# Extra rows of an expert in two parts of 64 rows instead of four of 32, and no branch prefetch

## The chip, the cores and the metric

The kernel runs on one core of one Trainium2 chip. Its time is the device time of one launch in microseconds; a smaller one is better. The engines are named as in the profile: PE is TensorE's matrix work, PEld its loads of stationary operands, DVE is VectorE, ACT is ScalarE, POOL is GpSimd, SP is the queue that issues most transfers. A `q` behind the name (PEq, PEldq) is the engine's sequencer, which reads the program, takes branches and waits on semaphores.

## The reference

One decoder block over 1024 tokens of width 1024, batch 1: a LayerNorm, three token mixers (gated DeltaNet, mLSTM, latent attention) that are gated, added and projected, a residual LayerNorm, and then a mixture of 16 experts with another residual LayerNorm. The change concerns the experts alone:

```python
scores = sigmoid(x_flat @ router_w)                 # 1024 tokens, 16 experts in 4 groups
# one group per token, the two best experts inside it; weights normalised over the two
for e in range(16):                                  # what routed_experts amounts to
    rows = tokens that chose e                       # as many as there are, no capacity
    y[rows] += w[rows, e] * ((silu(x[rows] @ w1[e]) * (x[rows] @ w3[e])) @ w2[e])
x = layer_norm(DEEPNORM_ALPHA * x + y)
```

There are 2048 pairs of token and expert, so an expert has 128 rows on average; w1 and w3 are 1024x512, w2 is 512x1024, all in float32.

## The kernel before

The front of the kernel (LayerNorm, mixers, merge, output projection, routing) takes the first 1380 us or so and is not touched, but for constants that `route_consts` prepares. Then `experts` runs over the experts in order, e = 0 to 15.

**Main rows.** The first 128 rows of an expert are one block. `turn_a` transposes the gathered rows `xg` and splits them in a high and a low half; `layer1` (8 steps c, one for each 128 inputs) multiplies them with w1 and w3, `layer2` (4 steps) with w2. Each step is six matmuls of 128x512 through `mm_pair` (L1571 to 1576). The weights come from memory by SP in tiles of 128x1024 (`Weights.load`), and ACT and DVE split each tile in a high and a low half (`split`, L1629 and L1630). Tiles are handed back as steps end, and that lets SP load the next.

**Extra rows.** Rows 128 to 255 of an expert are handled in parts of 32 rows, NM = 4 of them. The 32 rows are gathered as 128 lines of 256 numbers: partition 32q + r holds quarter q of row r (`quarters`, `gather` into `k.xm[:, m]`). `part_x` transposes them, `part_1` multiplies them in plain float32 with the unsplit weight tiles, `part_act` is the gate, `part_h` turns the result, `part_2` is the second layer, `part_y` scales and adds the rows to memory. In `part_1` and `part_2` a quarter of TensorE's columns (32 of 128) does a quarter of the output columns: four matmuls with the same 32-column stationary operand, 256 moving columns each, written to partitions 32q to 32q + 31 of the bank tile.

**Branches.** How many rows an expert has is known only at run time. `per_part` (L1696) reads the count once into a register (`count_of`, L1693) and nests one `If(count > 128 + 32 m)` per part, so the code of all four parts is in the program of every expert and what is not needed is jumped over. At the end of the nest the sequencer waits for its own engine. For `part_1` and `part_2` a hint (`ahead`, L1706) tells TensorE's sequencer ahead of time which way a branch will go.

**Order.** The order on PE, DVE and ACT is written by hand in the tables AT0 (expert 0), AT (1 to 14) and LAST (the last two): at step c of expert e, after that step's matmuls, the listed functions are called. In AT, `part_1(e)` comes at step 0, `turn_a(e+1)` and `part_2(e-1)` at step 3 (and there `ahead_1` of e + 1, which is the first to read that expert's count), `part_h(e)` at 4, `part_y(e-1)` at 5, `part_x(e+1)` at 8. POOL's order in this phase is the planner's.

Of the kernel before, what the change touches and what calls it, by code (L numbers as in the profile page):

```python
# [19 lines left out]
P = 128  # L20
# [1271 lines left out]
NE = 16  # L1292
NM = 4
CAPA = 2 * P
# [19 lines left out]
def route_consts(k, pool):  # L1314
# [10 lines left out]
    k.sc = pool.tile([P, NB, NE], F32, name="sc")  # L1325
    k.xm = pool.tile([P, NM, 2 * P], F32, name="xm")
    io = k.xm[:, 0]
    nc.gpsimd.iota(io, pattern=[[1, 2 * P]], base=1, channel_multiplier=0, allow_small_or_imprecise_dtypes=True)
# [12 lines left out]
    nc.gpsimd.memset(k.rowmul[:, 0:1], 1.0)  # L1341
    nc.gpsimd.memset(k.rowmul[:, 1:], 4.0)
    nc.gpsimd.memset(k.rowadd[:, 0:1], 0.0)
    for q in range(4):
        nc.gpsimd.memset(k.rowadd[32 * q:32 * q + 32, 1:], float(q))
    nc.vector.tensor_scalar(k.trash[:, 0:1], pc, float(T), None, op0=OP.add)
    nc.vector.tensor_scalar(k.trash[:, 1:], k.rowadd[:, 1:], -128.0, 4.0 * T, op0=OP.mult, op1=OP.add)
    nc.vector.scalar_tensor_tensor(k.trash[:, 1:], pc.to_broadcast([P, NM]), 4.0, k.trash[:, 1:], op0=OP.mult,
                                   op1=OP.add)
    k.past = pc  # L1350
    nc.vector.tensor_scalar(pc, pc, float(NE * CAPA + 1), None, op0=OP.add)
    k.spread = pool.tile([P, NM, 4, 32], BF, name="spread")
    nc.gpsimd.tensor_copy(k.spread, k.identb.rearrange("p (m r) -> p m r", r=32)[:, :, None, :].to_broadcast(
        [P, NM, 4, 32]))
    blank = k.xm[:, 1].bitcast(I32)[:, :NE * CAPA // P * 4].rearrange("p (j c) -> p j c", c=4)
# [167 lines left out]

def quarters(x):
    return x.rearrange("t (q n) -> (t q) n", q=4)

# [155 lines left out]
def experts(k, ws):  # L1682
# [4 lines left out]
    A = {}  # L1687
    xq, rq = quarters(k.x1), quarters(k.x1r)

# [5 lines left out]

    def per_part(e, fn, eng=nc.tensor, name=None):  # L1696
        count = count_of(e, eng)
        with ExitStack() as st:
            for m in range(NM):
                label = f"{name}_{e}_{m}" if name else None  # L1700
                st.enter_context(tc.If(count > P + 32 * m, label=label))
                if name and m + 1 < NM:
                    ahead(e, name, m + 1)
                fn(m)

    def ahead(e, name, m=0):  # L1706

        tc.mark_branch_hint_location(f"{name}_{e}_{m}", hint=count_of(e, nc.tensor) > P + 32 * m, engines=[ENG.PE])

    def look():  # L1710

        t = k.oh.rearrange("p b n -> p (b n)").bitcast(I32)
        t0 = t[:, :NE * 4].rearrange("p (e c) -> p e c", c=4)
        tq = t[:, NE * 4:NE * 4 * (1 + NM)].rearrange("p (e m c) -> p e m c", m=NM, c=4)
        ds = [nc.sync.dma_start(t0, k.table[:NE * CAPA].rearrange("(e s) c -> s e c", s=CAPA)[:P])]
        for q in range(4):
            for m in range(NM):
                ds.append(nc.sync.dma_start(tq[32 * q:32 * q + 32, :, m], k.table[:NE * CAPA].rearrange(
                    "(e s) c -> s e c", s=CAPA)[P + 32 * m:P + 32 * m + 32]))
        for d in ds:  # L1720
            for w in k.written:
                tc.add_manual_dep(d.ins, w.name, mybir.DependencyInfo(mybir.DependencyClass.Sync,
                                                                      mybir.DependencyReason.DATA),
                                  reason="the table is whole")
        A["table"] = t0, tq, t[:, NE * 4 * (1 + NM):NE * (4 + 6 * NM)].rearrange("p (i e m) -> p e m i", i=2, m=NM)

    def looked():
        t0, tq, iq = A["table"]
        nc.vector.tensor_scalar(iq, tq[:, :, :, 0:2], 4.0, k.rowadd[:, 1:2], op0=OP.mult, op1=OP.add)
# [33 lines left out]
    with tc.tile_pool(name="moe", bufs=2) as pool:  # L1763
        ws.late = pool
        ws.more(k.xsp, ["xs6", "xs7"], 0)
        ws.more(pool, [f"wl_{i}" for i in range(NSLOT - NEARLY - NB)], 0)
        bank = k.pe.tile([P, NM, 512], F32, name="bank")

# [41 lines left out]
        def part_x(e):  # L1810
            a = A[e]

            def turn(m):
                for j in range(2):
                    nc.tensor.transpose(bank[:, m, 256 + j * P:256 + j * P + P], k.xm[:, m, j * P:j * P + P], k.ident)

            per_part(e, turn)
            a.xT = pool.tile([P, NM, 256], F32, name="xmT")
            nc.scalar.activation(a.xT, bank[:, :, 256:], AF.Copy)

        def part_1(e):
            a = A[e]
            keys = [(e, 1, c) for c in range(KD)]
            w = [t.rearrange("p (i q n) -> p i q n", i=2, q=4) for t in ws.whole(keys)]

            def mul(m):
                for c, t in enumerate(w):
                    x = a.xT[:, m, c % 2 * P + c // 2 * 32:c % 2 * P + c // 2 * 32 + 32]
                    for q in range(4):
                        nc.tensor.matmul(bank[32 * q:32 * q + 32, m, 0:256], x, t[:, :, q], start=(c == 0),  # L1830
                                         stop=(c == KD - 1))

            per_part(e, mul, name="p1")
            ws.dropped(keys)

        def part_act(e):
            a = A[e]
            a.hm = pool.tile([P, NM, P], F32, name="mhm", bufs=1)
            silu_mul(k, a.hm, bank[:, :, 0:P], bank[:, :, P:2 * P])

        def part_h(e):
            a = A[e]
            per_part(e, lambda m: nc.tensor.transpose(bank[:, m, 0:P], a.hm[:, m], k.ident))
            a.hT = pool.tile([P, NM, P], F32, name="hmT", bufs=1)
            nc.scalar.activation(a.hT, bank[:, :, 0:P], AF.Copy)

        def part_2(e):
# [4 lines left out]
            def mul(m):  # L1852
                for c in range(4):
                    for q in range(4):
                        nc.tensor.matmul(bank[32 * q:32 * q + 32, m, 256:], a.hT[:, m, 32 * c:32 * c + 32],
                                         w[c][:, 256 * q:256 * q + 256], start=(c == 0), stop=(c == 3))

            per_part(e, mul, name="p2")
            ws.dropped(keys)

        def part_y(e):
            a = A[e]
            o = pool.tile([P, NM, 256], F32, name="mom", bufs=1)
            nc.vector.tensor_tensor(o, bank[:, :, 256:], bc(a.wq, 256), OP.mult)
            per_part(e, lambda m: add_rows(k, rq, a.rq[:, m:m + 1], o[:, m]), nc.gpsimd)

        def last_two(d, e):
# [13 lines left out]
            def whole():  # L1881
                s, bs = norm.tile(), norm.tile(12)
                for i in range(2):
# [9 lines left out]
                   "part_h": lambda: part_h(e), "part_2": lambda: part_2(e), "part_y": lambda: part_y(e),  # L1893
                   "ahead_1": lambda: ahead(e, "p1"), "ahead_2": lambda: ahead(e, "p2"),
                   "ahead_d": lambda: ahead(d, "p2"), "split": lambda: ws.split(min(1, ws.loaded - ws.made)), "layer1": lambda: mul(layer1, e), "act": lambda: act(e),
                   "turn2": lambda: turn2(e), "layer2": lambda: mul(layer2, e, False),
                   "consts": lambda: norm.consts(ws.spare), "gather": lambda: gather(k, z, k.x1r, a.i0), "whole": whole}
            for name in LAST.split():
# [8 lines left out]
               "part_1": part_1, "part_act": part_act, "part_h": part_h, "part_2": part_2, "part_y": part_y, "act": act,  # L1907
               "turn2": turn2, "ahead_1": lambda n: ahead(n, "p1"), "ahead_2": lambda n: ahead(n, "p2")}

# [5 lines left out]
        with tc.manual_schedule(engines=MANUAL):  # L1915
# [6 lines left out]
            for m in range(NM):  # L1922
                nc.scalar.activation(bank[:, m].rearrange("p (c n) -> p c n", n=P), bh(k.ident, 4), AF.Copy, scale=0.0)
            for e in range(NE - 1):
# [11 lines left out]

AT0 = ((-1, "mark", 1), (0, "find", 1), (1, "part_x", 0), (1, "ahead_1", 0), (2, "found", 1), (2, "fetch", 1),
       (2, "part_1", 0), (2, "ahead_1", 1), (5, "part_act", 0), (6, "part_h", 0),
       (7, "act", 0), (7, "turn_a", 1), (7, "part_x", 1), (6, "look", 0), (8, "looked", 0),
       (8, "fetch", 2))  # L1940
# [137 lines left out]
MIX_SCALE = ()  # L2078
LAST = """turn2_d split part_1 ahead_d split*2 part_2_d split part_y_d ahead_2 split part_act layer2_d*2 split part_h split part_2
layer2_d part_y layer2_d layer1*2 consts split*3 layer1*2 load7 split*2 load6 layer1 load0 load4 load3  # L2080
# [385 lines left out]
```

## Time and profile before

| | us |
|---|---|
| median of 3 runs | 1889.41 (1887.40 to 1893.02) |
| profiled execution | 1894.58 |
| its span, first to last instruction | 1892.8 |
| PE busy over the span | 1705.7 (90%) |
| DVE, ACT, POOL busy | 1130.4, 694.5, 384.3 |
| mean granted clock of TensorE | 0.956 of full |

The profiled execution is 1.8 us longer than its span and 5.2 us over the median of the runs. Busy time is a mean over stages: the experts' stage begins near 1380 us and is read in stretches of its own, each from the first layer-1 matmul of one expert to that of another. A branch counts as busy for no engine; its time shows as idle time of PE with the sequencer named as what ended it, or with `issue`, when the profile shows nothing that was waited for.

### The profile page before, as it was taken

Reading aid. Unit: us, or ns where it says so; the run is one execution under the profiler, and the core shown is the slowest. Engines: PE = TensorE matmul, PEld = TensorE weight load, DVE = VectorE, ACT = ScalarE, POOL = GpSimd, SP = SyncE. Lnnn points to the kernel's source line nnn. Section 1 sums busy time; section 2 is a strip of 40 time slices with the busy share of each in tenths; the row PEclk is TensorE's granted clock in tenths of the full one; section 3 lists DMA queues with packets and bytes.
Section 4 is the critical chain, followed back from the end, with each engine's and each line's share of the span. In section 5 each row is a group of like instructions: output and inputs, shape, how many; then the busy total and the mean of one; then the engine's idle time right before and its main releaser. Section 6 shows DMA issues by size and latency. Waiting matters only on the chain. (4 is left out here: it accounts for less than half of the span.)

```text
span 1892.8 us, 28732 instructions
## 1 busy us (share of the span) xinstructions
PE 1705.7 (90%) x10550; PEld 1434.4 (76%) x10550; DVE 1130.4 (60%) x2124; ACT 694.5 (37%) x1157; POOL 384.3 (20%) x419
## 2 busy tenths in 40 slices
PE   6999999999999999999999899979658888889872
PEld 5978988999998888888777788869535556667651
DVE  7685554464455524444576647765855556889766
ACT  6222222112211223345344522212134445778653
POOL 3140212113211005532100200120052212211115
PEclk9999999999999999999999999989879998999996
DMA  7222532323332225442200355371657677999835
GB/s 241 90 90 100 160 121 92 125 87 115 91 106 85 90 80 172 134 128 107 63 13 18 128 178 192 99 219 68 215 153 239 196 230 218 330 312 372 300 96 200
DMA packets 225793, 286.55 MB, mean 151 GB/s; under 512 B 48495, under 2 KB 153961, under 8 KB 225609
## 3 DMA queue, kind: packets, MB, share of 16 engines
q1 hardware_dynamic: 216792, 258.58, 41.4%
q0 software_dynamic: 8816, 25.47, 5.5%
q8 instruction: 122, 2.00, 0.5%
q14 instruction: 63, 0.51, 0.1%
HBM read 214.81 MB, written 69.17 MB: 150 GB/s over the span
## 5 line engine op out<-in xcount | busy, mean ns | idle before, releaser
L360 PE MATMUL psp<-xH,wh 128*128 128x512 f32 x704 | 285.0, 405 | 0.0
L361 PE MATMUL psp<-xL,wh 128*128 128x512 f32 x704 | 274.7, 390 | 3.9 <-POOL ci L509 2.2
L362 PE MATMUL psp<-xH,wl 128*128 128x512 f32 x704 | 276.0, 392 | 0.0
L360 PE MATMUL psp<-wh,xH 128*128 128x256 f32 (+1 forms) x576 | 165.7, 288 | 0.0
L362 PE MATMUL psp<-wh,xL 128*128 128x256 f32 (+1 forms) x576 | 162.4, 282 | 0.0
L361 PE MATMUL psp<-wl,xH 128*128 128x256 f32 (+1 forms) x576 | 162.4, 282 | 0.0
L361 PEld LDWEIGHTS psp<-xL,wh 128*128 128x128 f32 x704 | 132.6, 188 | 30.7 <-POOL ci L509 2.6
L362 PEld LDWEIGHTS psp<-xH,wl 128*128 128x128 f32 x704 | 132.1, 188 | 29.3
L360 PEld LDWEIGHTS psp<-xH,wh 128*128 128x128 f32 x704 | 132.7, 188 | 24.2
L1575 PE MATMUL ph<-wl,xgH 128*128 128x512 f32 x274 | 89.3, 436 | 39.4 <-issue 25.8
L360 PEld LDWEIGHTS psp<-wh,xH 128*128 128x128 f32 x576 | 110.5, 192 | 0.2
L361 PEld LDWEIGHTS psp<-wl,xH 128*128 128x128 f32 x576 | 110.5, 192 | 0.1
L362 PEld LDWEIGHTS psp<-wh,xL 128*128 128x128 f32 x576 | 110.3, 192 | 0.0
L346 DVE TENSOR_TENSOR wl<-wr,wh 128x1024 fp32r<-128x1024 f32 (+1 forms) x62 | 76.0, 1244 | 52.9 <-ACT wh L345 40.9
L1575 PEld LDWEIGHTS ph<-wl,xgH 128*128 128x128 f32 x274 | 54.4, 207 | 57.4 <-issue 38.4
L345 ACT ACTIVATE wh<-wr 128x1024 fp32r<-128x1024 f32 (+1 forms) x62 | 64.0, 1048 | 75.1 <-PE psp L361 51.3
L360 PE MATMUL pwo<-woh,mH 128*128 128x256 f32 x256 | 75.7, 296 | 14.2 <-DVE xs L2182 14.1
L360 PE MATMUL pbr<-yH,brh 128*128 128x512 f32 x192 | 76.5, 398 | 0.5 <-ACT ay L1249 0.5
L361 PE MATMUL pbr<-yL,brh 128*128 128x512 f32 x192 | 76.3, 397 | 0.0
L362 PE MATMUL pbr<-yH,brl 128*128 128x512 f32 x192 | 76.0, 396 | 0.0
L362 PE MATMUL pwo<-woh,mL 128*128 128x256 f32 x256 | 74.0, 289 | 0.0
L361 PE MATMUL pwo<-wol,mH 128*128 128x256 f32 x256 | 74.0, 289 | 0.0
(856 smaller groups left out, 4092.2 us busy)
## 6 DMA issues: line engine op xcount, KB each, us to landing
wl<-in_moe_w_dram SPq DMA_DIRECT2D x126, 256.0 KB
wr<-in_w_in_dram SPq DMA_DIRECT2D x60, 512.0 KB
xs<-in_moe_w_dram SPq DMA_DIRECT2D x82, 256.0 KB
wl<-in_moe_w_dram SPq DMA_DIRECT2D x34, 512.0 KB
gates<-gt SPq DMA_DIRECT2D x24, 512.0 KB
mgt<-gates SPq DMA_DIRECT2D x48, 256.0 KB
we<-in_moe_w_dram SPq DMA_DIRECT2D x48, 256.0 KB
we<-in_moe_w_dram SPq DMA_DIRECT2D x18, 512.0 KB
```

The source lines that it names most:

```text
L345: k.nc.scalar.activation(h, raw, AF.Copy)
L346: k.nc.vector.tensor_sub(l, raw, h)
L360: k.nc.tensor.matmul(out, aH, bH, start=start, stop=False)
L361: k.nc.tensor.matmul(out, aH, bL, start=False, stop=False)
L362: k.nc.tensor.matmul(out, aL, bH, start=False, stop=stop)
L1575: k.nc.tensor.matmul(ps, xL if p == 2 else xH, wl if p == 1 else wh, start=first and p == 0, stop=last and p == 2)
```

## The change

Parts of 64 rows, two of them (NM = 2, R = 64 rows, WP = 512 numbers of a row per line). The 64 rows are gathered as 128 lines of 512 numbers, half q of row r on partition 64q + r. In `part_1` and `part_2` half of TensorE's columns does half of the output columns: two matmuls with a 64-column stationary operand and 512 moving columns each. `part_x` transposes four blocks a part instead of two, `part_h` two instead of one. The bank tile, the gathered tile and the evictions have the same number of elements in all. `ahead` and its entries in the tables go, and with them the hints; the count of an expert is then first read in `part_x`. `look`, which reads the table of rows back, issues 4 transfers instead of 16 beside its first one.

```diff
-NM = 4
+NM = 2
+R = 128 // NM
+WP = 1024 // NM
@@ per_part
-    def per_part(e, fn, eng=nc.tensor, name=None):
+    def per_part(e, fn, eng=nc.tensor):
         count = count_of(e, eng)
         with ExitStack() as st:
             for m in range(NM):
-                label = f"{name}_{e}_{m}" if name else None
-                st.enter_context(tc.If(count > P + 32 * m, label=label))
-                if name and m + 1 < NM:
-                    ahead(e, name, m + 1)
+                st.enter_context(tc.If(count > P + R * m))
                 fn(m)
-
-    def ahead(e, name, m=0):
-
-        tc.mark_branch_hint_location(f"{name}_{e}_{m}", hint=count_of(e, nc.tensor) > P + 32 * m, engines=[ENG.PE])
@@ experts
-        bank = k.pe.tile([P, NM, 512], F32, name="bank")
+        bank = k.pe.tile([P, NM, 2 * WP], F32, name="bank")
@@ part_x
-                for j in range(2):
-                    nc.tensor.transpose(bank[:, m, 256 + j * P:256 + j * P + P], k.xm[:, m, j * P:j * P + P], k.ident)
+                for j in range(WP // P):
+                    nc.tensor.transpose(bank[:, m, WP + j * P:WP + j * P + P], k.xm[:, m, j * P:j * P + P], k.ident)
@@ part_1
-                    x = a.xT[:, m, c % 2 * P + c // 2 * 32:c % 2 * P + c // 2 * 32 + 32]
-                    for q in range(4):
-                        nc.tensor.matmul(bank[32 * q:32 * q + 32, m, 0:256], x, t[:, :, q], start=(c == 0),
+                    x = a.xT[:, m, c % (KD // NM) * P + c // (KD // NM) * R:][:, :R]
+                    for q in range(NM):
+                        nc.tensor.matmul(bank[R * q:R * q + R, m, 0:WP], x, t[:, :, q], start=(c == 0),
                                          stop=(c == KD - 1))
-            per_part(e, mul, name="p1")
+            per_part(e, mul)
@@ part_h
-            per_part(e, lambda m: nc.tensor.transpose(bank[:, m, 0:P], a.hm[:, m], k.ident))
+
+            def turn(m):
+                for j in range(WP // 2 // P):
+                    nc.tensor.transpose(bank[:, m, j * P:j * P + P], a.hm[:, m, j * P:j * P + P], k.ident)
+
+            per_part(e, turn)
@@ part_2
-                    for q in range(4):
-                        nc.tensor.matmul(bank[32 * q:32 * q + 32, m, 256:], a.hT[:, m, 32 * c:32 * c + 32],
-                                         w[c][:, 256 * q:256 * q + 256], start=(c == 0), stop=(c == 3))
-            per_part(e, mul, name="p2")
+                    for q in range(NM):
+                        nc.tensor.matmul(bank[R * q:R * q + R, m, WP:], a.hT[:, m, c % (4 // NM) * P + c // (4 // NM) * R:][:, :R],
+                                         w[c][:, WP * q:WP * q + WP], start=(c == 0), stop=(c == 3))
+            per_part(e, mul)
@@ the tables
-AT = ((0, "part_1", 0), (0, "turn2", -1), (0, "ahead_2", -1), (1, "part_act", 0), (3, "turn_a", 1), (3, "part_2", -1),
-      (3, "ahead_1", 1), (4, "part_h", 0), (5, "part_y", -1), (7, "act", 0),
+AT = ((0, "part_1", 0), (0, "turn2", -1), (1, "part_act", 0), (3, "turn_a", 1), (3, "part_2", -1),
+      (4, "part_h", 0), (5, "part_y", -1), (7, "act", 0),
       (8, "part_x", 1), (9, "fetch", 2))
...
```

AT0 and LAST lose their `ahead` entries in the same way, and the constants of `route_consts`, `look` and `looked` follow NM and R.

## Rows read from the trace of the kernel before

**Rows 1.** Busy time by stretch: expert 0, 1 to 5, 6 to 13, 11 alone, 14 to 15.

```profile
core 0: us, PE busy (x) PEld busy (x) DVE busy (x) ACT busy (x) POOL busy (x), PEclk, DMA share, GB/s
1381.90:1418.20 36.30, 23.42 (x148) 15.65 (x148) 17.70 (x33) 16.40 (x22) 21.77 (x20) 0.80 0.48 99
1418.20:1601.30 183.10, 151.57 (x1209) 107.23 (x1210) 98.42 (x103) 84.57 (x105) 39.15 (x24) 0.92 0.73 219
...
1601.30:1776.50 175.20, 156.27 (x708) 119.59 (x707) 155.25 (x161) 136.15 (x169) 33.43 (x19) 0.98 0.99 339
1714.00:1734.50 20.50, 18.96 (x86) 14.56 (x85) 19.32 (x21) 17.05 (x22) 3.82 (x2) 1.00 1.04 370
1776.50:1837.10 60.60, 42.91 (x309) 29.60 (x308) 34.69 (x35) 27.75 (x35) 7.05 (x4) 0.89 0.51 141
```

**Rows 2.** Waits, 1380 to 1837 us: total us, times, longest us.

```profile
PE ph L1575 <- issue: 29.6, 8, 10.2
PE phT L1550 <- PEq L1698: 16.2, 9, 4.4
...
PE ph L1575 <- PEq L1698: 7.9, 9, 3.6
PE py L1575 <- PEq L1698: 7.7, 8, 4.4
```

**Rows 3.** Branches of L1698 in four stretches: ns min/median/max, first and last start.

```profile
L1698 PEldq COMPARE_BRANCH  x70: 65/176/5262, 1419.2 to 1599.5; - x70
...
L1698 PEldq COMPARE_BRANCH  x18: 82/318/5643, 1605.4 to 1692.0; - x18
...
L1698 PEldq COMPARE_BRANCH  x12: 252/405/526, 1697.6 to 1753.5; - x12
...
L1698 PEldq COMPARE_BRANCH  x21: 70/181/5432, 1780.2 to 1831.8; - x21
```

**Rows 4.** Timeline of PE, part_1 of expert 1: start us, us, what, how many.

```profile
1420.00 1.50 PE L1830 MATMUL bank<-xs,xmT 128*32 128x256 f32 x24
1421.32 2.34 PE L1830 MATMUL bank<-wl,xmT 128*32 128x256 f32 x40
1423.48 1.48 PE L1830 MATMUL bank<-xs,xmT 128*32 128x256 f32 x24
```

**Rows 5.** L1830 alone: expert 1, expert 3, all; then L1855, all; L1815.

```profile
1418.20:1455.40 37.20, 7.11 (x128) 4.06 (x128) 0.91 0.78 236
1492.10:1533.10 41.00, 10.96 (x192) 6.93 (x192) 0.92 0.66 190
...
1381.90:1837.10 455.20, 42.51 (x704) 23.14 (x704) 0.93 0.78 245
...
1381.90:1837.10 455.20, 21.26 (x352) 10.95 (x352) 0.93 0.78 245
...
L1815 PE MATMUL bank<-ident,xm x22: 270/272/273, 1387.1 to 1804.8; 128*128 128x128 f32 x22
```

**Rows 6.** Timeline: the gap behind part_2 in expert 10; the count's load.

```profile
1701.99 0.72 PE L1575 MATMUL ph<-wl,xgH 128*128 128x512 f32 x2 [1.14 <-ACT xgH L1556]
...
L1693 PEldq TENSOR_LOAD <-cnt x16: 306/312/499, 1385.5 to 1794.7; - x16
```

**Rows 7.** Timeline of PE around branches: a short gap, four matmuls at either clock.

```profile
1414.69 0.73 PE L1575 MATMUL ph<-we,xgH 128*128 128x512 f32 x2 [0.43 <-PEq L1698]
...
1436.67 1.18 PE L1575 MATMUL ph<-wl,xgH 128*128 128x512 f32 x4 [1.50 <-issue]
...
1442.17 2.07 PE L1575 MATMUL ph<-wl,xgH 128*128 128x512 f32 x4 [3.64 <-PEq L1698]
...
1650.01 1.09 PE L1550 MATMUL phT<-ident,mhh 128*128 128x128 f32 x4 [2.84 <-PEq L1698]
```

**Rows 8.** DMA queue of TensorE's program: packets, MB, share of 16 engines.

```profile
q8 instruction: 122, 2.00, 0.5%
```

**Rows 9.** Timeline of POOL: the gathers for expert 1.

```profile
1406.92 1.85 POOL L1529 DMA_INDIRECT xm<-x,idx  x1 [0.30 <-issue]
1409.08 0.95 POOL L1529 DMA_INDIRECT xg<-x,idx  x1 [0.31 <-issue]
```

More of the change, by code (lines that the diff above doesn't have):

```diff
@@ L1341, in route_consts @@
     nc.gpsimd.memset(k.rowmul[:, 0:1], 1.0)
[L1342 removed]
+    nc.gpsimd.memset(k.rowmul[:, 1:], float(NM))
     nc.gpsimd.memset(k.rowadd[:, 0:1], 0.0)
[L1344 to L1345 removed]
+    for q in range(NM):
+        nc.gpsimd.memset(k.rowadd[R * q:R * q + R, 1:], float(q))
     nc.vector.tensor_scalar(k.trash[:, 0:1], pc, float(T), None, op0=OP.add)
[L1347 to L1348 removed]
+    nc.vector.tensor_scalar(k.trash[:, 1:], k.rowadd[:, 1:], -128.0, float(NM * T), op0=OP.mult, op1=OP.add)
+    nc.vector.scalar_tensor_tensor(k.trash[:, 1:], pc.to_broadcast([P, NM]), float(NM), k.trash[:, 1:], op0=OP.mult,
                                    op1=OP.add)
@@ L1521, in places, with pieces @@
     yield idx, w
-def quarters(x):
-    return x.rearrange("t (q n) -> (t q) n", q=4)
+def pieces(x):
+    return x.rearrange("t (q n) -> (t q) n", q=NM)
 def gather(k, x, src, idx):
@@ L1687, in experts @@
     A = {}
-    xq, rq = quarters(k.x1), quarters(k.x1r)
+    xq, rq = pieces(k.x1), pieces(k.x1r)
     def count_of(e, eng):
@@ L1715, in look @@
         ds = [nc.sync.dma_start(t0, k.table[:NE * CAPA].rearrange("(e s) c -> s e c", s=CAPA)[:P])]
-        for q in range(4):
+        for q in range(NM):
             for m in range(NM):
-                ds.append(nc.sync.dma_start(tq[32 * q:32 * q + 32, :, m], k.table[:NE * CAPA].rearrange(
-                    "(e s) c -> s e c", s=CAPA)[P + 32 * m:P + 32 * m + 32]))
+                ds.append(nc.sync.dma_start(tq[R * q:R * q + R, :, m], k.table[:NE * CAPA].rearrange(
+                    "(e s) c -> s e c", s=CAPA)[P + R * m:P + R * m + R]))
         for d in ds:
@@ L1728, in looked @@
         t0, tq, iq = A["table"]
-        nc.vector.tensor_scalar(iq, tq[:, :, :, 0:2], 4.0, k.rowadd[:, 1:2], op0=OP.mult, op1=OP.add)
+        nc.vector.tensor_scalar(iq, tq[:, :, :, 0:2], float(NM), k.rowadd[:, 1:2], op0=OP.mult, op1=OP.add)
         for e in range(2, NE):
@@ L1823, in part_1 @@
             keys = [(e, 1, c) for c in range(KD)]
-            w = [t.rearrange("p (i q n) -> p i q n", i=2, q=4) for t in ws.whole(keys)]
+            w = [t.rearrange("p (i q n) -> p i q n", i=2, q=NM) for t in ws.whole(keys)]
             def mul(m):
                 for c, t in enumerate(w):
-                    x = a.xT[:, m, c % 2 * P + c // 2 * 32:c % 2 * P + c // 2 * 32 + 32]
-                    for q in range(4):
-                        nc.tensor.matmul(bank[32 * q:32 * q + 32, m, 0:256], x, t[:, :, q], start=(c == 0),
+                    x = a.xT[:, m, c % (KD // NM) * P + c // (KD // NM) * R:][:, :R]
+                    for q in range(NM):
+                        nc.tensor.matmul(bank[R * q:R * q + R, m, 0:WP], x, t[:, :, q], start=(c == 0),
                                          stop=(c == KD - 1))
-            per_part(e, mul, name="p1")
+            per_part(e, mul)
             ws.dropped(keys)
@@ L1853, in mul @@
                 for c in range(4):
-                    for q in range(4):
-                        nc.tensor.matmul(bank[32 * q:32 * q + 32, m, 256:], a.hT[:, m, 32 * c:32 * c + 32],
-                                         w[c][:, 256 * q:256 * q + 256], start=(c == 0), stop=(c == 3))
-            per_part(e, mul, name="p2")
+                    for q in range(NM):
+                        nc.tensor.matmul(bank[R * q:R * q + R, m, WP:], a.hT[:, m, c % (4 // NM) * P + c // (4 // NM) * R:][:, :R],
+                                         w[c][:, WP * q:WP * q + WP], start=(c == 0), stop=(c == 3))
+            per_part(e, mul)
             ws.dropped(keys)
@@ L1893, in last_two @@
                    "part_h": lambda: part_h(e), "part_2": lambda: part_2(e), "part_y": lambda: part_y(e),
-                   "ahead_1": lambda: ahead(e, "p1"), "ahead_2": lambda: ahead(e, "p2"),
-                   "ahead_d": lambda: ahead(d, "p2"), "split": lambda: ws.split(min(1, ws.loaded - ws.made)), "layer1": lambda: mul(layer1, e), "act": lambda: act(e),
+                   "split": lambda: ws.split(min(1, ws.loaded - ws.made)), "layer1": lambda: mul(layer1, e), "act": lambda: act(e),
                    "turn2": lambda: turn2(e), "layer2": lambda: mul(layer2, e, False),
@@ L1907, in experts @@
                "part_1": part_1, "part_act": part_act, "part_h": part_h, "part_2": part_2, "part_y": part_y, "act": act,
-               "turn2": turn2, "ahead_1": lambda n: ahead(n, "p1"), "ahead_2": lambda n: ahead(n, "p2")}
+               "turn2": turn2}
         def events(table, e, c):
@@ L1922, in experts @@
             for m in range(NM):
-                nc.scalar.activation(bank[:, m].rearrange("p (c n) -> p c n", n=P), bh(k.ident, 4), AF.Copy, scale=0.0)
+                for i in range(0, 2 * WP, 512):
+                    nc.scalar.activation(bank[:, m, i:i + 512].rearrange("p (c n) -> p c n", n=P), bh(k.ident, 4), AF.Copy,
+                                         scale=0.0)
             for e in range(NE - 1):
@@ L1934, in experts @@
             last_two(NE - 2, NE - 1)
-AT0 = ((-1, "mark", 1), (0, "find", 1), (1, "part_x", 0), (1, "ahead_1", 0), (2, "found", 1), (2, "fetch", 1),
-       (2, "part_1", 0), (2, "ahead_1", 1), (5, "part_act", 0), (6, "part_h", 0),
+AT0 = ((-1, "mark", 1), (0, "find", 1), (1, "part_x", 0), (2, "found", 1), (2, "fetch", 1),
+       (2, "part_1", 0), (5, "part_act", 0), (6, "part_h", 0),
        (7, "act", 0), (7, "turn_a", 1), (7, "part_x", 1), (6, "look", 0), (8, "looked", 0),
        (8, "fetch", 2))
-AT = ((0, "part_1", 0), (0, "turn2", -1), (0, "ahead_2", -1), (1, "part_act", 0), (3, "turn_a", 1), (3, "part_2", -1),
-      (3, "ahead_1", 1), (4, "part_h", 0), (5, "part_y", -1), (7, "act", 0),
+AT = ((0, "part_1", 0), (0, "turn2", -1), (1, "part_act", 0), (3, "turn_a", 1), (3, "part_2", -1),
+      (4, "part_h", 0), (5, "part_y", -1), (7, "act", 0),
       (8, "part_x", 1), (9, "fetch", 2))
@@ L2078 @@
 MIX_SCALE = ()
-LAST = """turn2_d split part_1 ahead_d split*2 part_2_d split part_y_d ahead_2 split part_act layer2_d*2 split part_h split part_2
+LAST = """turn2_d split part_1 split*2 part_2_d split part_y_d split part_act layer2_d*2 split part_h split part_2
 layer2_d part_y layer2_d layer1*2 consts split*3 layer1*2 load7 split*2 load6 layer1 load0 load4 load3
```

26 lines of the change are left out of this document (13 added, 13 removed).

## The prediction

> **What bounds the kernel now.** I cut the experts' stage into stretches and read the busy times of each [rows 1]. In an expert without extra rows (expert 11) PE works 18.96 us of 20.50; DVE, at 19.32 us, is as full, and the transfers run at 370 GB/s. Experts 1 to 5 all have extra rows: 183.1 us, 36.6 each, while DVE works only 98.4 us in all and the transfers are at 219 GB/s. There PE alone sets the pace, with 151.6 us of work and 31.5 us of idle time. So in these stretches, and in the last two experts (17.7 us idle in 60.6), a microsecond of PE's work or idle time is a microsecond of the kernel.
>
> The waits tell what the idle time is [rows 2]. The lines ended by PEq L1698, the sequencer at a branch, make 16.2 + 7.9 + 7.7 = 31.8 us, and 29.6 us are "issue", the longest 10.2 us: nothing was waited for, PE had no instruction. The branches themselves show it [rows 3]: the median is 0.2 to 0.4 us, but the longest in three of four stretches take 5.3, 5.6 and 5.4 us, whereas in 1693 to 1755 none is over 0.53. A branch lands either on code that is there or on code that must be fetched; the second costs some 5 us of the sequencer. Part of that is covered, because the sequencer runs ahead of PE: the branch of 5.64 us left PE idle for 2.84 [rows 3, 7]. I put the stalls down to jumps over long code. One part is 64 loads and 64 matmuls in part_1 (704 matmuls for 11 parts [rows 5]) and half of that in part_2, so an expert without extra rows jumps over 512 and 256 instructions. With the change these are 128 and 64.
>
> **The change, term by term.** The sum is made on the profiled execution, 1894.6 us.
>
> *PE's work in the parts.* Line 1830 has 704 matmuls; 64 are one part (128 in expert 1, 192 in expert 3), and line 1815's 22 transposes, two a part, agree: 11 parts, two in expert 1, three in expert 3, six single ones [rows 5]. In parts of 64 rows, expert 1 needs one and expert 3 two: 9. A part of part_1 takes 3.48 us, from 1420.00 to 1423.48 for 64 matmuls [rows 4], that is 0.218 us for each four, though one lasts 0.38: the four quarters run side by side. A part after has 32 matmuls of 512 columns; if two halves run side by side, 16 pairs at twice 0.218 us make 6.96 us. Part_2 is half of it: 1.74 us, then 3.48. So 9 x (6.96 + 3.48) = 94.0 us, with 0.3 us a part for the ends of the two groups 96.7, against the measured 42.51 + 21.26 = 63.8 [rows 5]: +33. Transposes: 14 more in part_x and 7 more in part_h at about 0.11 us spacing make +2. Expert 0's share (6.96 + 0.2 after, 5.8 before) goes into its own term, which leaves **+34**. A 64-column matmul with two halves is not in the trace. The nearest row from below is the quarters' (the 34), from above the same matmuls one behind the other, as if halves did not overlap: 94 us more. I take the former, since what keeps four groups of columns going at once is the same thing.
>
> *Idle time of experts 1 to 5 and of the last two.* With a jump of 64 or 128 instructions where there were up to 512, I expect landings to be as in 1693 to 1755. Then an expert with parts keeps about 0.4 us from the reference expert (1.54 less the 1.14 of the next term) and two or three gaps like the 0.43 us behind part_h [rows 1, 6, 7], 1.5 in all: 31.5 - 5 x 1.5 = **-24**. In the last two, part_1 and part_2 have three such stalls of up to 4.4 us [rows 2]; 17.7 falls to some 6.7: **-11**. The price of a landing is bounded by rows at 0.25 and 5.64 us; I take the lower end, with 1 us a part of slack.
>
> *Experts 6 to 13.* Idle time is 175.2 - 156.3 = 18.9 us [rows 1], of which eight times the reference's 1.54 is 12.3; the other 6.6 are missed landings and should go. In the reference 1.14 us is one gap [rows 6]: behind part_2 the sequencer reads the next expert's count for the hint, and that load alone is 0.31 us of it. The trace names ACT as releaser, but the gap is there in each such expert, with the same count load in it. The change moves the load to part_x, where the sequencer is ahead of six matmuls (1.4 us), so it is hidden; if PE were out of matmuls there, it costs its 0.9 again. Eight times 0.9 would be 7 us; but DVE needs 19.32 us an expert, and the transfers are at 370 GB/s, so only part can be had. I take 4.5. Together **-11**.
>
> *Clock.* [...] Granted clock short of 1 times length is 0.08 x 183.1 + 0.02 x 175.2 + 0.11 x 60.6 = 24.8 us [rows 1], some of it in idle time. With the long gaps gone I take back less than half: **-11**, with 0 and 20 as bounds.
>
> *Expert 0.* 10.2 us of stall follow its part_1 [rows 2], but what comes behind is bound elsewhere: expert 1's rows are gathered at 1409.08, behind POOL's writes of the row table and two part gathers [rows 9]. One of those two goes (expert 1 then has one part), so the gather starts 2.2 us earlier. I take **-4**.
>
> *At nothing.* The evictions have as many elements as before. Gathers and additions move 128 lines of 2 KB in 9 parts for 1 KB in 11, under 3 MB more in 455 us at 245 GB/s [rows 5]. `look` issues 12 transfers fewer on SP ahead of weight loads, which in expert 1 are not what PE waits for. If that cover goes, all three are in favour of the change or under 3 us.
>
> Sum: 34 - 24 - 11 - 11 - 11 - 4 = -27. The profiled 1894.6 becomes 1868; on the median of the runs, 5.2 us lower, **1862 us**.
>
> The program of TensorE is fetched in 122 packets of 2.00 MB [rows 8], 16 KB each. [...]
>
> **Rivals.**
> *Landings still miss, and now nothing is hinted* (slower). Its place is the two jumps of every expert. For it: most experts' jumps hit with hints in 1693 to 1755, and no row shows a long jump without one. Against it: the jumps are a quarter as long, and branches of part_x and part_h, never hinted, are mostly among the short ones. Price: the idle and clock terms (-24, -11, -11 for missed landings and clock, and -6.6) stay away, and 16 unhinted jumps in experts 6 to 13 at up to 2.84 us add some 25: 1889 + 34 + 25 - 8 = about 1940 at full strength; it turns the sign when more than half of the landings miss. At three quarters, 1915.
> *Half of the landings miss or come late*: gains and work cancel, 1886 to 1892.
> *The halves don't run side by side*: 94 us more, 1862 + 94 = 1956. Against it: the quarters do.
> *DVE and the transfers set the floor sooner*, so that experts 1 to 5 gain two thirds and 6 to 13 only the missed landings: 1862 + 15 = 1877. For it: 370 GB/s and 19.32 of 20.50 us of DVE in experts without parts; against it: 219 GB/s in those with parts.
>
> **How the numbers follow.** Forecast 0.60 (own range 1845 to 1876: the clock at its bounds of 20 and 0, the slack unused or doubled); sooner floor 0.14; cancelled 0.09; missed landings 0.13; halves in turn 0.04. A difference of 0.3%, 5.7 us, is what this measurement can tell from none. Faster: 0.60 + 0.14 = 0.74; same 0.09; slower 0.17. The range runs from 1838 to 1902: it leaves out the halves in turn, most of the missed landings and 0.05 below.
>
> **What would show it.** Right: line 1830 with 32 x 9 = 288 matmuls of 128x512, in pairs 0.43 us apart, 6.9 us a part; no branch of L1698 over some 2 us; fewer packets in q8 (a fifth less or more); idle time of experts 1 to 5 near 8 us, granted clock there near 1; expert 3, alone with two parts, still the longest. Wrong: pairs 0.86 us apart (halves in turn), branches of 4 to 6 us in experts without parts (unhinted landings), or the reference expert at 20.5 us as before (the count load was not what the gap was).

## The result, and the profile after

| | before | after |
|---|---|---|
| median, us | 1891.22 (1887.40 to 1895.53, 4 runs) | 1858.52 (1857.02 to 1860.43, 4 runs) |
| ratio, 95% interval | | 0.9829 (0.9801 to 0.9857) |
| profiled execution, its span | 1894.6, 1892.8 | 1860.4, 1858.7 |
| mean granted clock | 0.956 | 0.970 |

The kernel became 32.7 us faster by the medians, 34.1 by the two profiled spans; 1862 was forecast. The helpers' lines shift by two: L1575 and L1698 of before are L1577 and L1700 after. Part_1's L1830 is now L1825, and L1855 is still part_2.

The busy times by stretch of the kernel after answer to [rows 1]: experts 0, 1 to 5, 6 to 13, 11 alone and 14, and then the tail, which holds expert 15. The columns are the same: length, busy time of each engine, granted clock, share of the DMA engines, GB/s.

```profile
1379.90:1415.10 35.20, 24.62 (x117) 15.58 (x117) 19.03 (x32) 16.57 (x22) 22.09 (x19) 0.84 0.56 109
1415.10:1585.70 170.60, 163.95 (x740) 97.67 (x741) 96.19 (x100) 84.51 (x105) 34.04 (x20) 0.98 0.77 237
1585.70:1746.30 160.60, 155.26 (x693) 117.89 (x692) 154.04 (x161) 136.24 (x169) 36.30 (x19) 1.00 1.02 356
1687.20:1706.60 19.40, 18.80 (x85) 14.52 (x84) 18.99 (x21) 16.97 (x21) 3.87 (x2) 1.00 1.04 368
1746.30:1799.00 52.70, 48.13 (x217) 26.88 (x216) 34.60 (x35) 27.75 (x34) 5.45 (x3) 1.00 0.65 209
1799.00:1858.70 59.70, 21.46 (x77) 16.08 (x75) 34.21 (x38) 22.64 (x34) 30.32 (x25) 0.68 0.50 172
```

The tail of the kernel before, from the same view, stands against the last of these lines:

```profile
1837.10:1892.80 55.70, 20.05 (x77) 15.05 (x75) 34.23 (x38) 22.62 (x34) 28.25 (x24) 0.68 0.50 180
```

Read PE's busy time and the length together. Experts 1 to 5 have 12.4 us more of PE's work than before and still take 12.5 us less: their idle time fell from 31.5 to 6.6 us. Experts 6 to 13 lost 14.6 us, expert 14 7.9, expert 0 1.1, and the stage began 2.0 us earlier; the tail took 4.0 us more. Together 12.5 + 14.6 + 7.9 + 1.1 + 2.0 - 4.0 = 34.1. The 2.0 us of the earlier start are no effect of the change that the runs can tell: in the thirteen profiles of this document the stage begins between 1373.8 and 1381.9 us, behind the same front.

PE's waits of the kernel after from 1380 to 1799 us (total us, times, longest us) answer to [rows 2]:

```profile
PE pxg L1547 <- DMA xg<-x,idx: 8.8, 1, 8.8
PE ph L1577 <- PEq L1700: 5.1, 12, 0.4
PE py L1577 <- PEq L1700: 3.1, 7, 0.5
PE phT L1552 <- PEq L1700: 2.2, 5, 0.4
```

The lines of "issue" are gone, and what is left behind branches is 0.4 us a time. One new wait heads the list, 8.8 us for the gather of expert 1's rows; it stands in expert 0. The branches of the kernel after, all together (ns, min/median/max), and its count loads, for [rows 3, 6]:

```profile
L1700 PEldq COMPARE_BRANCH  x128: 65/179/925, 1384.4 to 1795.9; - x128
...
L1695 PEldq TENSOR_LOAD <-cnt x16: 302/306/493, 1383.5 to 1764.9; - x16
```

The longest branch took 0.93 us where it was 5.64. The timeline of PE after: part_1 of expert 1, and expert 11 at the place where expert 10 had its 1.14 us gap [rows 4, 6]:

```profile
1417.93 4.28 PE L1825 MATMUL bank<-xs,xmT 128*64 128x512 f32 x12
1422.04 4.46 PE L1825 MATMUL bank<-wl,xmT 128*64 128x512 f32 x20
...
1693.53 1.04 PE L1547 MATMUL pxg<-ident,xg 128*128 128x128 f32 x8
1694.71 0.70 PE L1577 MATMUL ph<-wl,xgH 128*128 128x512 f32 x2
```

Behind the transposes, which end at 1694.57, the next matmul starts 0.14 us later. The whole of L1825, the whole of L1855, and L1825 in expert 3 alone (length, PE busy, PEld busy), for [rows 5]:

```profile
1379.90:1799.00 419.10, 65.05 (x288) 20.31 (x288) 0.98 0.83 268
...
1379.90:1799.00 419.10, 32.67 (x144) 9.66 (x144) 0.98 0.83 268
...
1481.70:1519.60 37.90, 13.96 (x64) 4.50 (x64) 1.00 0.68 204
```

Expert 3's 64 matmuls in 13.96 us are 32 pairs at 0.436 us: the halves do run side by side. Expert 1's part, shown above, took 8.57 us instead of 6.98, because its first matmuls, up to 1420.9 us, ran at a granted clock of 0.50 behind the new wait of 8.8 us; from there it was 1.00. And the queue that carries the programs, for [rows 8]:

```profile
q8 instruction: 91, 1.49, 0.3%
```

### The profile page after: what moved, and what is told of

It is laid out like the page before. It is cut to its first block, busy times and chain, and to the rows that moved or that the text cites. A ratio compares the mean times of both kernels' runs of the same rounds, so it can differ in the third digit from the quotient of the medians.

```text
span 1858.7 us, 27306 instructions
## 1 busy us (share of the span) xinstructions
PE 1722.1 (93%) x9941; PEld 1418.5 (76%) x9941; DVE 1126.9 (61%) x2124; ACT 694.9 (37%) x1157; POOL 382.3 (21%) x413
## 5 line engine op out<-in xcount | busy, mean ns | idle before, releaser
L1577 PE MATMUL ph<-wl,xgH 128*128 128x512 f32 x274 | 80.9, 401 | 4.8 <-PEq L1700 3.0
L1577 PEld LDWEIGHTS ph<-wl,xgH 128*128 128x128 f32 x274 | 49.5, 188 | 23.0 <-issue 10.5
```

What stands on the lines that cost most here:

```text
L1577: k.nc.tensor.matmul(ps, xL if p == 2 else xH, wl if p == 1 else wh, start=first and p == 0, stop=last and p == 2)
```

## The experiments

Eleven kernels, each built on the kernel after unless said otherwise, and timed against the kernel before in the same session (its medians there were 1892.7, 1892.1 and 1894.3 us). None leaves work out. The diffs are shortened. The theory (A) was the prediction's: short jumps land on code that is there, so the hints have nothing left to do. The rival: the parts' new shape is worth little, and what counts is that the hints and their count loads are gone.

**The hints put back, and the count alone.** What theory B of the first expectation calls the forward fetch shows in the trace of the kernel before: from 1693 to 1755 us, where every branch is short [rows 3], q8 brought 9 packets while PE worked 57.35 of the 62.0 us. First the kernel after with hints at the places where before had them:

```diff
+    st.enter_context(tc.If(count > P + R * m, label=label))    # and ahead(e, name, m + 1)
-AT = ((0, "part_1", 0), (0, "turn2", -1), (1, "part_act", 0), ...
+AT = ((0, "part_1", 0), (0, "turn2", -1), (0, "ahead_2", -1), (1, "part_act", 0), ... (3, "ahead_1", 1), ...
```

> The changed kernel with the hints put back (same places as before, for parts of 64 rows). Theory A (the distance of the landing decides; a hint only mends long jumps, and costs the count load behind part_2): no branch over 2 us comes or goes, the gap of 1.1 us behind part_2 is back, expert 11 takes 20.4 us instead of 19.46, the time is 1858.5 + 14 x 0.9 = 1871 us (1866 to 1875). Theory B (the hints themselves caused the missed landings, by taking the place of the forward fetch): branches of 4 to 6 us are back in some ten places, 1880 to 1890 us.

Then no hints, but the count read where the hint had it read, behind part_2:

```diff
+      (3, "count", 1),      # in AT, and (2, "count", 1) in AT0
```

> The changed kernel without hints, but with the count of the next expert read where the hint had it read, behind part_2 at step 3. If the count load is what the gap of 1.14 us was: expert 11 takes 20.3 us instead of 19.46 and the time is 1858.5 + 14 x 0.85 = 1870 us, within 3 us of the run with hints. If the gap was the hint, or the ACT instruction that the trace names as releaser: 1858.5 +- 3 us, expert 11 at 19.5.

Measured: 1887.23 us with hints (1883.61 to 1891.33; ratio to before 0.9978, 0.9955 to 1.0001) and 1870.54 with the count alone (1869.81 to 1871.28; 0.9883, 0.9836 to 0.9930). So the count's place is worth 12.0 us, as expected, and the hints themselves another 16.7, which theory A had at nothing; the two were expected within 3 us of each other. The time with hints lies in theory B's range, but without B's sign: two branches are over 1 us, not ten. The branches with hints (ns, min/median/max):

```profile
L1700 PEldq COMPARE_BRANCH  x128: 65/212/7153, 1384.7 to 1823.9; - x128
```

In the trace of the count alone, the gap stands again behind the transposes in expert 11:

```profile
1700.86 1.03 PE L1547 MATMUL pxg<-ident,xg 128*128 128x128 f32 x8
1702.78 0.73 PE L1577 MATMUL ph<-wl,xgH 128*128 128x512 f32 x2 [0.88 <-ACT xgH L1558]
```

ACT is named, but the count load is what the edit put there. And the kernel with hints, timeline of PE in experts 6, 7 and 13:

```profile
1590.89 0.63 PE L1577 MATMUL ph<-xs,xgH 128*128 128x512 f32 x2
1594.95 1.22 PE L1577 MATMUL ph<-wl,xgL 128*128 128x512 f32 x2 [3.43 <-issue]
...
1630.16 1.22 PE L1577 MATMUL ph<-we,xgH 128*128 128x512 f32 x2 [5.06 <-issue]
...
1754.16 0.39 PE L1577 MATMUL ph<-xs,xgH 128*128 128x512 f32 x1 [3.10 <-issue]
```

Two of these stalls, at 1591 and 1751, stand in the middle of a row of matmuls with no branch between them, 14 and 13 matmuls behind the landing of a short branch; PE waited for nothing that the profile shows. The third, of 5.06 us, follows the branch of 7.15 us, the longest in any run here. The two matmuls behind the first stall take 1.22 us where two took 0.63 before it, and the mean granted clock from 1585.7 to 1613 us was 0.87. These three experts take 18.0 us more than in the kernel with the count alone (30.81 + 26.51 + 25.92 against 24.05 + 20.29 + 20.88), which is the whole of the 16.7. So with the hints PE ran dry, for 5.06 us at a landing and for 3.43 and 3.10 us in code that follows in order. What the hints do to cause it, no run shows.

**Long code back, without hints.** Copies of the second part that never run (they stand under a branch on more rows than there are) lengthen the jump from 128 and 64 instructions (layer 1 and 2) to 512 and 256; a later kernel has two copies, for 256 and 128:

```diff
-            for m in range(NM): ...
+            if pad:                                  # pad=6, later pad=2
+                st.enter_context(tc.If(count > P + R * NM))
+                for _ in range(pad):
+                    fn(1)
```

> The changed kernel with code that is never run appended inside part_1 and part_2 of each expert (six more copies of a part's matmuls under a condition that no expert meets), so that what is jumped over is 512 and 256 instructions again, without hints; the work done is the same. Theory A: most landings miss, branches of 4 to 6 us in experts with and without parts, 16 experts x 2 jumps at 1.2 to 2.8 us of PE idle time each, 1858.5 + 38 to 90, centre 1910 us. Theory B (no hints, so no misses): 1858 to 1862 us.

> The kernel after, with code added behind the second part that never runs (it stands under a branch on more rows than any expert has), so that the untaken part is 256 instructions of TensorE for layer 1 and 128 for layer 2: twice the kernel after's 128 and 64, and half of what the run with 512 and 256 had. A (how far the branch jumps decides whether its landing has to wait for an instruction fetch): the cost lies between the kernel after's 1858.5 us and the 1922 us of that run. If it grows with the length, (256 - 128)/(512 - 128) of the 63.5 us: +21, so 1880 us (1868 to 1897), with some of the branches over 1 us and some not. A2 (there is an edge, and it lies above 256): 1858 to 1862 us and no branch over 1 us. A3 (the edge lies between 128 and 256): 1905 us or more and about as many branches over 1 us as in that run (25). B (what cost there was not the length of the jump but something else of the added code): no order by length; above 1922 us or below 1857 us.

And the kernel before with its quarters but without hints:

> The kernel before (four parts of 32 rows in quarters) with the hints taken out, so the count is first read in part_x. Theory A: jumps over 512 and 256 instructions now miss without a hint; against the changed kernel 33 us less work in the parts and 16 x 2 landings at 1.2 to 4.4 us: 1825 + 50 to 100, centre 1890 us. Theory B: the misses go with the hints, 1826 to 1835 us.

| kernel | jumped over | median us | branches over 1 us, sum | packets in q8 |
|---|---|---|---|---|
| after | 128, 64 | 1858.52 | 0 | 91 |
| after, longer | 256, 128 | 1865.94 (1862.95 to 1868.36) | 5, 19.5 us | 104 |
| after, longest | 512, 256 | 1922.05 (1917.03 to 1923.01) | 25, 115.1 us | 126 |
| before, no hints | 512, 256 | 1900.14 (1893.97 to 1904.90) | 24, 94.2 us | 129 |
| before | 512, 256 | 1891.22 | 17, 62 us | 122 |

The branch lines of the longest, the longer, and the quarters without hints (ns, min/median/max):

```profile
L1700 PEldq COMPARE_BRANCH  x130: 65/188/6307, 1383.0 to 1852.0; - x130
```

```profile
L1700 PEldq COMPARE_BRANCH  x128: 65/184/5608, 1379.5 to 1800.6; - x128
```

```profile
L1698 PEldq COMPARE_BRANCH  x140: 65/176/6542, 1383.9 to 1834.1; - x140
```

Nothing else was changed in the first three kernels than code that never runs, and the time follows its length: the longer jump is the cause. Where a landing falls in the packets of 16 KB in which q8 brings the code [rows 8] moves with the length too, and no run varies that alone. The growth isn't even. The first 128 added instructions cost 7.4 us, where a straight line through the ends gives 21; the next 256 cost 56. The expectation of 1880 missed, and so did the edge above 256; 1922 and 1900 lie in theory A's ranges (1896 to 1948, 1875 to 1925). Without any hint, the longest kernel also has three stalls amid rows of matmuls, 3.18, 2.09 and 3.83 us, 3 to 11 matmuls behind a landing; the first:

```profile
1647.51 2.08 PE L1577 MATMUL ph<-wl,xgH 128*128 128x512 f32 x4 [3.18 <-issue]
```

What a miss looks like, PE of the kernel with 256 in expert 7:

```profile
1605.19 0.62 PE L1577 MATMUL ph<-wl,xgL 128*128 128x512 f32 x2
1608.59 0.63 PE L1552 MATMUL phT<-ident,mhh 128*128 128x128 f32 x4 [2.78 <-PEq L1700]
1608.97 1.59 PE L1577 MATMUL ph<-we,xgH 128*128 128x512 f32 x4
1610.36 1.05 PE L1577 MATMUL ph<-we,xgL 128*128 128x512 f32 x2
```

2.78 us idle, and then two matmuls in 1.05 us instead of 0.62; in the kernel before, two matmuls took 1.05 us at a granted clock of 0.50 (1408.73) and 0.62 at 1.00 (1412.17). That expert took 23.70 us against 19.48, so this landing cost 4.2 us.

The two changes crossed, in medians: with quarters, hints save 7 us net of their count gap (1900.1 to 1892.7, the kernel before in the same session); with halves they cost 29 (1858.5 to 1887.2). The parts alone are worth 42 us without hints, and some 4 with them, where the interval of the ratio reaches 1. Neither edit brings the gain by itself.

**Where the rest went: expert 0 and the tail.** In expert 0 the stall behind part_1 (10.2 us, [rows 2]) went, but the timeline of PE after shows a wait of nearly its size a little later:

```profile
1402.38 0.63 PE L1577 MATMUL ph<-we,xgL 128*128 128x512 f32 x2
1411.78 1.94 PE L1547 MATMUL pxg<-ident,xg 128*128 128x128 f32 x8 [8.76 <-DMA xg<-x,idx]
```

and POOL has that gather behind the last table write and the part's gather, for [rows 9]:

```profile
1402.94 1.75 POOL L1470 DMA_INDIRECT table<-trib,cum  x1 [0.30 <-issue]
1405.00 0.99 POOL L1531 DMA_INDIRECT xm<-x,idx  x1 [0.30 <-issue]
1406.30 0.96 POOL L1531 DMA_INDIRECT xg<-x,idx  x1 [0.30 <-issue]
```

So half of the table writes were put behind the gathers:

```diff
-    for b in range(NB): for i in range(2): table write
+    for j in range(8): write(j)                 # route_table
+    with tc.issue_after(gather of xg, expert 1):
+        for j in range(8, 16): write(j)
-AT0: (8, "looked", 0), (8, "fetch", 2)
+AT0: (8, "fetch_x", 2)     AT of expert 1: (2, "looked", 0), (2, "fetch", 1)
```

> The kernel after, with the gather of expert 1's rows ahead of the last 8 of the 16 table writes in GpSimd's order, and the read of the table's parts moved from expert 0 to expert 1. A (in the kernel after, TensorE's wait of 8.76 us at turn_a of expert 1 stands there because the gather, issued at 1406.30, queues behind the table writes; it is the stall of the branch that comes back as a wait on a DMA): the gather is issued at about 1392, the wait goes, expert 0 takes some 27 us instead of 35.2, and the time is 1850 us (1848 to 1853). B (the table, and so expert 2's gather, is late instead: its last write goes out about 2.5 us later and expert 1 begins 8 us earlier): the wait reappears at turn_a of expert 2, 1855 to 1859 us. C (the stretch is bound by the splits of the weights on ScalarE and VectorE): 1856 to 1859 us with idle gaps before matmuls that read split weights.

Measured 1849.68 us (1848.36 to 1854.08; 0.9771, 0.9712 to 0.9829). Expert 0 takes 25.31 us against 35.19. The wait of 8.76 us is gone, and a new one of 1.3 us stands at turn_a of expert 2, the place that B named:

```profile
PE pxg L1554 <- DMA xg<-x,oh: 1.3, 1, 1.3
```

A held: the stall of the branch had become a wait on POOL's order.

In the tail PE waits longer for the last expert's rows than before; the waits there of the kernel before and of the kernel after:

```profile
PE phT L1550 <- DVE mhh L1568: 4.4, 1, 4.4
```

```profile
PE phT L1552 <- DVE mhh L1570: 9.3, 1, 9.3
```

The chain after it, by start times of single lines: POOL's adds, SP's first load of x1r, ACT's first statistics, ACT's part of `mhh`:

```profile
1799.06 1.55 POOL L1536 DMA_INDIRECT x1r<-mom,oh  x1 [8.15 <-DVE mom L1864]
1805.09 2.22 POOL L1536 DMA_INDIRECT x1r<-mo,oh  x1 [4.48 <-issue]
...
1811.65 0.33 SPq L2043 DMA_DIRECT2D spxs<-x1r  x1
...
1814.98 1.06 ACT L2048 ACTIVATE xm<-spxs 128x1024 f32<-128x1024 f32 x1 [10.92 <-DMA spxs<-x1r]
1817.31 0.57 ACT L1568 ACTIVATE mhh<-ph 128x512 f32<-128x512 f32 x1
```

From add to add it is 6.0 us, from add to load 6.6. The first add landed 4.8 us after its start, at 1803.9, and the last semaphore that POOL's queue passes before the second one is at 1804.0: the program lets the second wait for the first. The load seems to wait for the second add in the same way (from issue to landing such an add took 6.1 us in the run with another buffer below). Expert 15's first matmul comes 38.1 us earlier than before, at 1799.0, but these adds come only 34.2 earlier (1799.06 against 1833.26) and 33.5 (1805.09 against 1838.62). If the row norms bind the end, it hangs on the adds. Two edits tried to move it, another buffer for the last scaled rows, and the activation ahead of the statistics:

```diff
-o = pool.tile([P, NM, WP], F32, name="mom", bufs=1)
+o = ws.spare()                                            # last expert only
```

> The kernel after, with another buffer for the last expert's scaled rows, so that VectorE's product for them at 1797.56 need not wait 3.33 us until the add of the expert before it has left the one buffer. A (the end is now bound by the chain of adds into x1r, the loads of x1r behind them and the row norms, and no longer by TensorE): every step of that chain moves by up to 3.3 us, TensorE's wait of 9.3 us at turn2 of the last expert shrinks by as much, and the time is 1855 us (1854 to 1857). B (TensorE, or the row norms' own work, binds the end): nothing moves, 1857 to 1860 us.

```diff
-layer1*2 load5 layer1 stats7 load1 stats6 act scale6      # LAST
+layer1*2 load5 layer1 act stats7 load1 stats6 scale6
```

> The kernel after, with the activation of the last expert's first rows ahead of the statistics of rows 7 and 6 in ScalarE's and VectorE's order (in the kernel after it stands behind them, and they wait for loads of x1r). A (the end is bound by the chain of the row norms, which starts when the adds into x1r have landed; TensorE's wait of 9.35 us at turn2 of the last expert costs nothing): the wait shrinks to under 2 us and the time stays, 1857 to 1860 us. B (that wait is what the end gave back: TensorE's order binds): 1849 to 1853 us.

Measured: 1858.14 (1855.20 to 1859.65) and 1860.56 (1859.13 to 1862.25). Neither moved the time. With the other buffer POOL's two adds read:

```profile
1797.06 1.55 POOL L1536 DMA_INDIRECT x1r<-spwe,oh  x1 [6.46 <-DVE spwe L1864]
1804.30 1.55 POOL L1536 DMA_INDIRECT x1r<-mo,oh  x1 [5.69 <-ACT wl L1631]
```

The first add is 2.0 us earlier and the second only 0.8: the first took 6.1 us to its landing, at 1803.1, instead of 4.8. PE's wait shrank by 0.8 (9.3 to 8.5). That is theory A's direction, a quarter of its size, and in time less than the runs can tell from nothing. With the activation ahead, PE's waits in the tail were:

```profile
PE py L1577 <- ACT mhH L1563: 11.7, 1, 11.7
PE phT L1552 <- DVE mhh L1570: 2.1, 1, 2.1
```

The wait went down to 2.1 as expected and came back one operation later, since `mhH` still stands behind the statistics. The time fits A (the row norms bind), but as PE did not come forward the run does not exclude B; what binds the last 45 us is left open.

**A better cut.** A first part of 32 rows in quarters and a second of 64 in halves; no expert has more than 96 extra rows, and beyond that the kernel's overflow code takes over:

```diff
-NM = 2; R = 128 // NM; WP = 1024 // NM; CAPA = 2 * P
+NM = 2; RS = (32, 64); QS = (4, 2); OF = (0, 32); WP = 512; CAPA = P + 96
-            tc.If(count > P + R * m)
+            tc.If(count > P + OF[m])        # R, the pieces and the columns from RS[m], QS[m]
```

> The kernel after, with a first part of 32 rows in quarters of the columns and a second of 64 rows in halves (96 rows in all; no expert has more here): 192 instructions of layer 1 and 96 of layer 2 under the branches, no hints. Experts 0, 2, 4, 5, 14 and 15 need only the first, 1 and 3 both. A (the parts' matmuls bind experts 1 to 5 and 14): a part of 32 rows takes 3.5 + 1.7 us by the kernel before's rows and one of 64 6.9 + 3.65 by those of the kernel after; so -5.3 us for each of experts 2, 3, 4, 5, 14 and 15, +5.2 for expert 1, and nothing for expert 0, where TensorE waits for the gather anyway: -27, 1832 us (1826 to 1838). B (at 192 instructions some landings miss again): 10 to 20 us of branches over 1 us, 1840 to 1852 us. C (with TensorE shorter, the splits on VectorE bind experts 2, 4 and 5, and the adds the end): 1845 to 1855 us, no branch over 1 us, and idle gaps that VectorE or a DMA ends.

> The two edits that each gained, together: parts of 32 rows in quarters and 64 in halves, and expert 1's gather ahead of the last 8 table writes. A (the wait for the gather, 13.54 us in the mixed kernel, goes whole, as 9.9 us of expert 0 went in the kernel with the early gather alone, and 1.3 us come back at turn_a of expert 2): 1831.7 - 12 = 1820 us (1816 to 1824). B (TensorE now being some 13 us earlier, the read of the table, which comes no earlier, makes expert 2's gather late): the wait moves to expert 1, 1824 to 1831 us.

> The kernel with mixed parts and the early gather, with the activation of the last expert's first rows ahead of the rows' statistics. A (the row norms bind the end): as without that edit, 1820 us (1816 to 1824), within 1 us of it. B (TensorE binds the end): 6 to 9 us below it.

| kernel | median us | ratio to before, 95% |
|---|---|---|
| mixed parts | 1831.71 (1829.76 to 1834.62) | 0.9667 (0.9609 to 0.9725) |
| mixed, early gather | 1825.34 (1822.40 to 1828.24) | 0.9642 (0.9609 to 0.9675) |
| the same, activation ahead | 1824.20 (1823.76 to 1825.03) | 0.9636 (0.9606 to 0.9666) |

The mixed parts gave 27 us, the number of A, but not in A's places: experts 3, 4 and 5 took 5.3, 5.3 and 4.6 us less, 14 and 15 8.5 and 2.7; expert 1 took 1.7 less where A had 5.2 more, and experts 7 to 10 took 7.7 us more. No branch was over 0.45 us, yet PE ran dry behind them, as in expert 8:

```profile
1608.69 0.71 PE L1583 MATMUL ph<-wl,xgH 128*128 128x512 f32 x2
1611.07 0.61 PE L1583 MATMUL ph<-wl,xgH 128*128 128x512 f32 x2 [1.67 <-DVE mhL L1570]
```

DVE's `mhL` has no part in these matmuls; in the sister stalls of 1.25 and 1.70 us nothing is named at all. With 192 and 96 instructions no branch is long, but PE stands still in the code that follows the landing in order. In experts 7, 8 and 9 the stall stands 9, 6 and 3 matmuls behind the landing of the jump over part_1. Why it moves from expert to expert, no run shows. The early gather gave 6.4 us more, not 12: on the combined kernel PE still has this wait at turn_a of expert 1, because the gather, third in a row now, went out at 1394.32 and PE was ready by 1397.2.

```profile
PE pxg L1560 <- DMA xg<-x,idx: 4.7, 1, 4.7
```

B's number held, B's place (expert 2) did not. The activation ahead made no difference that the runs can tell.

## Why the prediction was right

| term | forecast | profiled |
|---|---|---|
| work of the parts, without expert 0's 1.3 | +34 | (65.1 + 32.7) - (42.5 + 21.3) + 2.0 of transposes - 1.3 = +35 |
| clock, the rest of PE's work | -11 | -18 |
| idle time, experts 1 to 5 | -24 | 6.6 - 31.5 = -25 |
| idle time, expert 14 | -11 | 4.6 - 17.7 = -13 |
| experts 6 to 13 | -11 | 5.3 - 18.9 = -14 |
| expert 0 | -4 | 35.2 - 36.3 = -1 |
| start of the stage | no term | 1379.9 - 1381.9 = -2 |
| tail | 0 | 59.7 - 55.7 = +4 |
| sum | -27 | -34 |

*The parts' work* was read from the quarters' rate, 0.218 us for four. The halves came to 0.436 for two, and all nine parts to 97.7 us where 96.7 was the sum. The bound from above, halves one behind the other, is excluded.

*Landings.* The step that carried the gain, jumps of 64 and 128 land as in 1693 to 1755, held: no branch over 0.93 us. The rival that they still miss is wrong for this length and right for four times it (25 misses, slower than before by 1.1 to 2.1%). That a long branch waits for code shows in the trace of the kernel before: each of its 17 branches over 1 us ends 1.36 to 1.54 us after a packet of q8 has landed. In the one of 5.64 us, from 1644.20 on, the packet came at 1647.32 and took 1.09 us; the queue in the time of that branch alone:

```profile
q8 instruction: 1, 0.02, 1.2%
```

*The count load* was most of the gap in the reference expert: put back alone, 0.88 of the 1.14 us are there again (with the hint 1.16), and it costs 12.0 us in all. I had allowed 4.5 of 7 because DVE would bind at 19.32 us an expert. That floor moved: in expert 11, now 19.4 us, DVE works 18.99, still as full as PE at 18.80, so which of the two holds the expert now is not shown. With the missed landings the term came to 14 instead of 11. The rival of a sooner floor is out with that.

*Clock.* In the trace of the kernel before the granted clock was 0.50 over the four matmuls behind the gap of 3.64 us [rows 7], and 1.00 over the four of 1436.67, behind 1.50 us. How much of the 24.8 us comes back when the long gaps go, no run shows alone; the sum took less than half of it. PE's busy time before expert 15 rose by 17.8 us (374.2 to 392.0), though the parts' own rose by 36: the rest of its work, the same matmuls, took 18 us less at a granted clock that is 0.98 in experts 1 to 5 and 1.00 behind them. This is the largest error of a term, inside its bounds of 0 and 20. Both errors went the same way, and the tail, which the sum had at nothing, took 4 us back. That the forecast is only 3.5 us off is in part luck. The sum fell 7 us short, 2 of them by the chance start of the stage, and the distance from the profiled execution to the median, taken as 5.2 us, came to 1.9, which hid 3.3 of it.

*What the prediction did not have*: it took the hints' removal as free apart from the count load. They cost 17 us with short code, so the jump's length and the hints had to change together. The argument "landings as good as the best stretch of before" was sound, but no row of before could show that the hints themselves stall. Nor was all of the 29.6 us of "issue" [rows 2] the jumps': three stalls, 12.7 us, follow branches of 3.0 to 5.3 us, but the longest, 10.2 us in expert 0, comes before the first branch over 1 us of the stage (at 1437.0). It went with the change; what made it is open.

## What to carry to other kernels

When a branch skips code that is unrolled in each iteration, count the instructions skipped: here no branch was over 0.93 us at 128, a miss at 256 cost 4 us, and at 512 there were 25 branches over 1 us in 16 experts, so shorter bodies that do more padded work (34 us more of PE here) can still win. Test prefetch hints by taking them out whenever the code they guard gets shorter (on jumps of 128 they cost 16.7 us here), and put count loads where the sequencer is ahead of its engine (12.0 us here). When a stall of the sequencer goes, read which queue is late next at that place: here a gather behind POOL's table writes took back most of it (8.8 of 10.2 us).

## What the runs showed of the hardware that was not expected

- Branch hints on jumps of 128 instructions cost 16.7 us: PE stood still for 3.4 and 3.1 us amid straight rows of matmuls, with nothing waited for that the profile shows, and for 5.1 us behind a branch of 7.15 us. Such stalls amid straight rows are not the hints' alone: at 512 without hints there were three, of 2.1 to 3.8 us.
- A missed landing cost more than its idle time: 2.78 us idle was 4.2 us in all, and the matmuls behind it were slower (1.05 us for two against 0.62).
- Between no cost and a missed branch there is a third case: at 192 instructions no branch is over 0.45 us, but PE runs dry for 1.25 to 1.7 us, 3 to 9 matmuls behind the landing.
- An indirect add of 128 lines to memory took 4.8 and 6.1 us from its start to its landing, and that is what the second add into the same tensor cost, for which the program has it wait: the two adds into x1r went out 6.0 and 7.2 us apart, though the second one's data were there earlier.
